# Scalar one-hots, fused sums of expert numbers and a different fill of the query stage, in a hybrid encoder block

## The chip, the cores and the metric

The kernel runs on one core of a Trainium2 chip. The metric is the device time of one execution in microseconds, the median of several runs. The engines go by the names of the profile: PE is TensorE (matmuls), DVE is VectorE, ACT is ScalarE, POOL is GpSimd, and SP issues transfers.

## What is computed

One encoder layer over 512 tokens of width 1024, in fp32:

```python
h = x + mixer(rmsnorm(x, norm_mix_g))       # HGRN2 and Hyena branches, projections, gates
h = h + peer_ffn(rmsnorm(h, norm_ffn_g))
out = rmsnorm(h, norm_final_g)

# peer_ffn, for a block xb of tokens: 8 heads, 2 x 128 sub-keys, 16384 experts
qh = (xb @ w_q).reshape(T, 8, 2, 128)
s = einsum('thpc,hpnc->thpn', qh, subkeys)
s1, i1 = top_k(s[:, :, 0], 16);  s2, i2 = top_k(s[:, :, 1], 16)
cand_s = s1[..., :, None] + s2[..., None, :]          # 256 candidates
cand_i = i1[..., :, None] * 128 + i2[..., None, :]
top_s, pos = top_k(cand_s, 16)
experts = take_along_axis(cand_i, pos);  g = softmax(top_s)
act = gelu(einsum('td,thkd->thk', xb, u_tab[experts])) * g
y = einsum('thk,thkd->td', act, v_tab[experts])
```

## The kernel before

A product of two fp32 matrices is made of three matmuls: each operand is split into a high part (ScalarE, L85) and the rest (a subtraction, L86, on VectorE or GpSimd).

The mixer comes first. `mixer` loads the four blocks of 128 tokens, normalises each (`token_rstd` on ScalarE, a multiplication by the reciprocal root and the weights `gm` on VectorE, L228), and `turn` transposes them with TensorE. `gm` holds the same 1024 weights on all 128 partitions, loaded by one broadcast transfer on SP's queue (L223). ScalarE's queue issues the small tables `vec` and `ident`, and the filter weights `fw3` (L455) and decay rates `decb` (L464) of the Hyena branch. Then follow the Hyena branch, the HGRN2 branch and the output projection, up to about 806 us.

The second half is PEER. Block 0 of the tokens (GTB) has its experts gathered row by row by GpSimd. The other three blocks (DTB) go through all 16384 experts: a row of 128 experts is multiplied with all 384 tokens (`act_row`: 24 matmuls, then gelu), weighted by a dense gate matrix, and multiplied with the same experts' outputs (`combine`: 18 matmuls). The stages are:

1. `queries` (16 halves of heads): a projection, the scores, the 16 best of 128 per token and half head on VectorE (`top16`).
2. `select` (called `chosen`), once for each block and half of the heads: 50 candidate pairs for each of four heads, their 16 best, a softmax, and the expert number of each of the 16 places. A place holds the position of a pair. The expert number is found by comparing the place with the list `pio` of the pairs' positions (L1188), multiplying the one-hot by the candidates' numbers (L1190), and summing (L1181). The first eight places can only be among the first 20 pairs. In steps of two heads this makes 12 wide operations a call. It yields after each step, with a cost that is used for interleaving.
3. `gates_out`, for each of the three blocks: with an expert number split into row and column, every token's 128 choices become two one-hots of 128 x 128, which TensorE multiplies into the token's part of the gate matrix. A batch is four tokens, 32 batches a block. `one` (L1228) compares for row and column at once, in bf16, ScalarE copies the rows in another order (L1230), `own` (L1231) multiplies the columns by the gates. The product goes through `Gs` to the memory `Gd`.
4. `rows`, the expert loop: 128 rows of combination, with the rest of the activation rows spread over the first 120, and the gathered block's choices and gathers (`gathered`) woven in.

Activation rows that are made before the loop ("fill") stay in a ring of 14 rows or, for KEPT pairs, go to memory (`kept`) and come back. There are 2 x KEPT + RING - LEFT of them: 27. In `queries`, two are run at its end. The others are woven into the choices and gate matrices by the yielded costs. Before the loop their low parts are subtracted on VectorE, in the loop on GpSimd (`looping`). In `queries` the first halves of two blocks' choices (EARLY) go along, one step per query from the ninth on, the rest at its end.

The order on each engine is made by a planner when the program is built: it takes instructions by their place in the program as soon as, by its own estimates, their inputs and buffers are there. `issue_after` puts instructions behind a given one on the same engine.

Of the kernel before, what the change touches and what calls it, by code (L numbers as in the profile page):

```python
# [21 lines left out]
P = 128  # L22
L = 512
D = 1024
# [134 lines left out]
def block_kernel(tc, a):  # L159

    nc = tc.nc
    with ExitStack() as ctx:
# [5 lines left out]
        nc.scalar.dma_start(vec, a["vec"])  # L168
# [3 lines left out]
        C = Ctx()  # L172
        C.nc, C.tc, C.a, C.ident, C.ones, C.vec, C.eps = nc, tc, a, ident, ones, vec, epsc
# [28 lines left out]
def mixer(C):  # L202
# [104 lines left out]
def hyena(C, ctx, xh, xl, raws, fill):  # L307
# [112 lines left out]
    for half in range(D // HC):  # L420
# [33 lines left out]
        for row in (0, FH):  # L454
            nc.scalar.dma_start(fw3[row : row + FH], a["f_w3"].rearrange("f (d c) -> f d c", d=2)[:, :, half * HC : half * HC + HC])  # L455
# [6 lines left out]
        for dr in range(2):  # L462
            o = dr * D + half * HC
            nc.scalar.dma_start(decb[:, dr], a["f_decay"][:, o : o + HC].to_broadcast([P, HC]))  # L464
        with tc.issue_after(C.turned):
            nc.scalar.activation(decb, decb, AF.Abs)
# [324 lines left out]
KEPT = 8  # L791
LEFT = 3
UB = 2
EARLY = 2
MIX = 3
STEPS = 1
# [13 lines left out]
def peer(C, ctx, mh, ml):  # L810
# [9 lines left out]
    pio = cp.tile([P, NPAIR, TOPK // 2], BF16, name="pio")  # L820
    with tc.tile_pool(name="pid", bufs=1) as ip:
        pid = ip.tile([P, NPAIR], F32, name="pid")
        nc.scalar.dma_start(pid, a["pair"].to_broadcast([P, NPAIR]))
        nc.vector.tensor_copy(pio, pid[:, :, None].to_broadcast([P, NPAIR, TOPK // 2]))
    iota = cp.tile([P, P, 4], BF16, name="iota")
    nc.gpsimd.iota(iota, pattern=[[1, P], [0, 4]], base=0, channel_multiplier=0, allow_small_or_imprecise_dtypes=True)  # L826
    gidx = cp.tile([P, P], I32, name="gidx")
    gdot = cp.tile([P, P], F32, name="gdot")
    gw = cp.tile([P, P], F32, name="gw")
    def chosen(pool, tb, part, ahead=2):  # L830
        return select(C, pool, tb, part, v16, i16, gate, eid, pio, ahead)
# [53 lines left out]
    with tc.tile_pool(name="slw", bufs=2) as sw, tc.tile_pool(name="gb", bufs=1) as gb, \  # L885
            tc.tile_pool(name="go", bufs=3) as go, tc.tile_pool(name="ps_g", bufs=5, space=PSUM) as ps_g:
        def main():
            rest = [[chosen(sw, tb, part) for part in range(2) if part or k >= EARLY] for k, tb in enumerate(DTB)]
            yield from chain(*rest[0])
            for k, tb in enumerate(DTB):  # L890
                nxt = chain(*rest[k + 1]) if k + 1 < len(DTB) else iter(())
# [245 lines left out]
def select(C, w2, tb, part, v16, i16, gate, eid, pio, ahead=2):  # L1137
# [59 lines left out]
    while found:  # L1197
        reduce()
# [170 lines left out]
```

## Time and profile before

| | us |
|---|---|
| median of 3 runs | 2113.68 (2111.99 to 2114.71) |
| the profiled execution | 2113.9 |
| its span, first to last instruction | 2112.1 |
| PE busy | 2058.7 |
| DVE busy | 1736.1 |
| ACT busy | 978.6 |
| POOL busy | 638.2 |

The span is one execution on the chip. Busy time of an engine is the time in which at least one of its instructions ran; the durations of matmuls are modelled, and a matmul's record overlaps the next, as do the records of VectorE. A timeline row begins with the start in us from the span's start and the time that the row covers; neighbouring instructions of one kind are merged to one row (x2). The difference of two starts is what an instruction costs in a row of others.

### The profile page before, as it was taken

What the parts mean: (1) busy time and instruction counts of PE and PEld (TensorE: products, weight loads), DVE (VectorE), ACT (ScalarE), POOL (GpSimd) and SP (SyncE); (2) the same over time, 40 slices, a digit from 0 to 9 for tenths busy, and PEclk for the clock granted to TensorE, in tenths of its full rate; (3) what the DMA queues carried; (4) which work ended last, traced back from release to release, by engine and by line L of the source; (5) the groups of instructions that cost most, each with busy time, mean ns of one, the idle gap of its engine ahead of it and who ended that gap; (6) DMA issues with size and microseconds to landing.
All of it is one profiled execution on the core that took longest, in us unless ns stands there. A gap on an engine that the chain in (4) does not pass through costs nothing. (4 is left out here: it accounts for less than half of the span.)

```text
span 2112.1 us, 29790 instructions
## 1 busy us (share of the span) xinstructions
PE 2058.7 (97%) x11109; PEld 1822.7 (86%) x11109; DVE 1736.1 (82%) x3073; ACT 978.6 (46%) x1396; POOL 638.2 (30%) x361
## 2 busy tenths in 40 slices
PE   7999999999999999979999999999999999999998
PEld 6888888888888898879988989989989998998997
DVE  6888764998998546999999988878878879778785
ACT  6555434667665623337766423333333333333333
POOL 0000000000000000000000378877777676666760
PEclk9999999999999999999999999999999999999999
DMA  6212222222212444124547689988888988888884
GB/s 199 80 51 66 70 70 94 67 65 66 70 54 81 120 151 139 61 70 168 202 180 250 192 311 344 327 318 304 321 318 301 317 311 299 316 317 324 296 286 148
DMA packets 153949, 407.68 MB, mean 193 GB/s; under 512 B 12457, under 2 KB 65451, under 8 KB 152140
## 3 DMA queue, kind: packets, MB, share of 16 engines
q1 hardware_dynamic: 110028, 255.98, 35.8%
q0 software_dynamic: 36864, 134.23, 17.6%
q10 hardware_dynamic: 6912, 15.56, 2.1%
q8 instruction: 87, 1.43, 0.3%
q14 instruction: 58, 0.48, 0.1%
HBM read 373.22 MB, written 32.51 MB: 192 GB/s over the span
## 5 line engine op out<-in xcount | busy, mean ns | idle before, releaser
L86 POOL TENSOR_TENSOR ul<-uraw,uh 128x1024 fp32r<-128x1024 f32 x100 | 265.3, 2654 | 589.7 <-DMA uraw<-in_uT 387.6
L95 PE MATMUL ps_a<-pxl,uh 128*128 128x384 f32 x1008 | 343.1, 340 | 0.0
L94 PE MATMUL ps_a<-pxh,uh 128*128 128x384 f32 x1008 | 341.8, 339 | 1.3 <-ACT gact L867 1.2
L980 PE MATMUL acc<-vl,gh 128*128 128x512 f32 x768 | 301.5, 393 | 2.1 <-DVE vl L86 2.1
L979 PE MATMUL acc<-vh,gh 128*128 128x512 f32 x768 | 299.7, 390 | 2.6 <-ACT vh L85 2.6
L981 PE MATMUL acc<-vh,gl 128*128 128x512 f32 x768 | 301.5, 393 | 0.0
L94 PE MATMUL ps_mm<-xh,whi 128*128 128x512 f32 (+1 forms) x656 | 259.1, 396 | 1.5 <-ACT xh L195 1.2
L940 DVE SCALAR_TENSOR_TENSOR xg<-grow,gw,xg 128x1024 f32<-128x1024 f32 x127 | 208.6, 1643 | 63.1 <-DMA grow<-in_v,gidx 62.0
L931 DVE SCALAR_TENSOR_TENSOR grow<-grow,xg 128x1024 f32<-128x1024 f32 x128 | 195.9, 1541 | 73.6 <-DMA grow<-in_u,gidx 73.3
L95 PE MATMUL ps_mm<-xl,whi 128*128 128x512 f32 (+1 forms) x656 | 255.0, 390 | 0.3 <-DVE xl L196 0.3
L85 ACT CAST vh<-vraw 128x1024 fp32r<-128x1024 f32 x128 | 134.3, 1050 | 252.7 <-PE acc L981 179.7
L826 POOL IOTA iota<- 128x512 bf16 x1 | 1.2, 1237 | 754.4 <-DVE gt L281 754.4
L906 POOL DMA_INDIRECT grow<-in_u,gidx x128 | 201.0, 1570 | 41.4 <-issue 19.4
L97 PE MATMUL ps_a<-pxh,ul 128*128 128x384 f32 x1008 | 200.1, 338 | 6.3 <-DVE ul L86 4.1
L85 ACT CAST uh<-uraw 128x1024 fp32r<-128x1024 f32 x128 | 134.7, 1053 | 143.5 <-PE ps_a L95 76.5
L94 PEld LDWEIGHTS ps_a<-pxh,uh 128*128 128x128 f32 x1008 | 191.1, 190 | 6.4 <-ACT gact L867 2.2
L95 PEld LDWEIGHTS ps_a<-pxl,uh 128*128 128x128 f32 x1008 | 190.9, 189 | 3.8
L86 DVE TENSOR_TENSOR vl<-vraw,vh 128x1024 fp32r<-128x1024 f32 x128 | 186.4, 1457 | 8.3 <-ACT vh L85 8.3
L97 PEld LDWEIGHTS ps_a<-pxh,ul 128*128 128x128 f32 x1008 | 176.8, 189 | 8.2 <-DVE ul L86 5.5
L906 POOL DMA_INDIRECT grow<-in_v,gidx x128 | 170.5, 1332 | 32.7 <-issue 18.3
L85 ACT CAST whi<-wraw 128x1024 fp32r<-128x1024 f32 x112 | 117.3, 1050 | 131.0 <-PE ps_mm L95 123.5
L980 PEld LDWEIGHTS acc<-vl,gh 128*128 128x128 f32 x768 | 144.6, 188 | 31.1 <-DVE vl L86 2.9
(414 smaller groups left out, 4188.8 us busy)
## 6 DMA issues: line engine op xcount, KB each, us to landing
uraw<-in_uT SPq DMA_DIRECT2D x128, 512.0 KB, 7.0
vraw<-in_v SPq DMA_DIRECT2D x128, 512.0 KB, 6.3
wraw<-in_w_in SPq DMA_DIRECT2D x80, 512.0 KB, 3.6
Gd<-Gs SPq DMA_DIRECT2D x12, 2048.0 KB, 7.2
gt<-Gd SPq DMA_DIRECT2D x32, 768.0 KB, 8.7
wraw<-in_w_q SPq DMA_DIRECT2D x16, 512.0 KB, 4.0
wraw<-in_w_b SPq DMA_DIRECT2D x8, 512.0 KB, 3.6
wraw<-in_w_a SPq DMA_DIRECT2D x8, 512.0 KB, 4.3
```

Of the source, the lines that this page charges most:

```text
L85: nc.scalar.copy(hi, src)
L86: return (eng or nc.vector).tensor_sub(lo, src, hi).ins
L94: nc.tensor.matmul(out, ah, bh, start=(i == 0), stop=False)
L95: nc.tensor.matmul(out, *((al, bh) if late else (ah, bl)), start=False, stop=False)
L97: nc.tensor.matmul(out, *((ah, bl) if late else (al, bh)), start=False, stop=(stop and i == n - 1))
L826: nc.gpsimd.iota(iota, pattern=[[1, P], [0, 4]], base=0, channel_multiplier=0, allow_small_or_imprecise_dtypes=True)
L906: nc.gpsimd.indirect_dma_start(out=t, out_offset=None, in_=tab, in_offset=bass.IndirectOffsetOnAxis(ap=gidx[:, j : j + 1], axis=0))
L931: nc.vector.scalar_tensor_tensor(t, t, 1.0, xg, op0=ALU.mult, op1=ALU.mult, accum_out=gdot[:, j : j + 1])
L940: nc.vector.scalar_tensor_tensor(gacc, t, gw[:, j : j + 1], gacc, op0=ALU.mult, op1=ALU.add)
L979: nc.tensor.matmul(acc[k][:, c], gh[:, ts_], vh[:, ds_], start=(r == 0), stop=False)
L980: nc.tensor.matmul(acc[k][:, c], gh[:, ts_], vl[:, ds_], start=False, stop=False)
L981: nc.tensor.matmul(acc[k][:, c], gl[:, ts_], vh[:, ds_], start=False, stop=(r == NK - 1))
```

## The change

The expert numbers are found by one operation for each of the 64 places of a call: it compares the list of positions with the place (a scalar per token, read through a pointer), multiplies by the candidates' numbers and sums. For that `pio` and `cpf` become fp32. In `gates_out` the bf16 compare is made for the rows alone, and the columns' one-hot times gate by one operation per token with two scalars per partition (number and gate), compared with `line`, the numbers 0 to 127.

KEPT is 10. `queries` runs an activation row after each query from the eighth on, with two choice steps, and takes the first halves of all three blocks. The part of `main` after it begins with the second half of the first block, its costs multiplied by 1.3.

The weights of the first normalisation come as one row of 4 KB on ScalarE's queue, and two matmuls with ones copy it to all partitions of two PSUM banks, from where VectorE reads it, in two halves. `vec` is issued after `ident`, and the transfers of `fw3` and `decb` after the last turned copy.

```diff
-        nc.scalar.dma_start(vec, a["vec"])
         nc.scalar.dma_start(ident, a["ident"])
+        C.fetch_vec = lambda: nc.scalar.dma_start(vec, a["vec"])
...
         log_table(C)
-        gm = n1.tile([P, D], F32, name="gm")
+        C.fetch_vec()
+        gm = n1.tile([1, D], F32, name="gm")
+        gps = [C.ps_x.tile([P, 512], F32, name="ps_x") for _ in range(2)]
...
-                nc.sync.dma_start(gm, a["g_mix"].to_broadcast([P, D]))
+                nc.scalar.dma_start(gm, a["g_mix"])
+                for c, pg in enumerate(gps):
+                    nc.tensor.matmul(pg, C.ones[0:1], gm[:, c * 512 : c * 512 + 512], start=True, stop=True)
...
-            nc.vector.scalar_tensor_tensor(xn, xn, rs, gm, op0=ALU.mult, op1=ALU.mult)
+            for c, pg in enumerate(gps):
+                xc = xn[:, c * 512 : c * 512 + 512]
+                nc.vector.scalar_tensor_tensor(xc, xc, rs, pg, op0=ALU.mult, op1=ALU.mult)
...
-        for row in (0, FH):
-            nc.scalar.dma_start(fw3[row : row + FH], ...)
+        with tc.issue_after(C.turned):
+            for row in (0, FH):
+                nc.scalar.dma_start(fw3[row : row + FH], ...)
...
-        for dr in range(2):
-            o = dr * D + half * HC
-            nc.scalar.dma_start(decb[:, dr], ...)
         with tc.issue_after(C.turned):
+            for dr in range(2):
+                o = dr * D + half * HC
+                nc.scalar.dma_start(decb[:, dr], ...)
...
-KEPT = 8
+KEPT = 10
+FIRSTC = 1.3
-EARLY = 2
-STEPS = 1
+STEPS = 2
...
-            rest = [[chosen(sw, tb, part) for part in range(2) if part or k >= EARLY] for k, tb in enumerate(DTB)]
-            yield from chain(*rest[0])
+            rest = [chosen(sw, tb, 1) for tb in DTB]
+            for c in rest[0]:
+                yield FIRSTC * c
...
-        early = chain(*(chosen(sw, tb, 0) for tb in DTB[:EARLY]))
+        early = chain(*(chosen(sw, tb, 0) for tb in DTB))
-            if hp > 7:
+            if hp >= HEADS - 1:
                 run(islice(early, STEPS))
+                next(fill)
...
-    for hd in range(0, H, H2):
-        for k0, n in ((0, NFIRST), (K2, NPAIR)):
-            one = w2.tile([P, H2, NPAIR, K2], BF16, name="one", bufs=2)
-            ex = w2.tile([P, H2, K2, NPAIR], F32, name="exp", bufs=ahead + 1)
-            nc.vector.tensor_tensor(one[:, :, :n], ..., op=ALU.is_equal)
-            nc.vector.tensor_mul(ex[:, :, :, :n], ...)
-            ...
-            yield 0.7 if k0 == 0 else 1.3
+    for hd in range(H):
+        for k in range(TOPK):
+            n = NFIRST if k < TOPK // 2 else NPAIR
+            own = w2.tile([P, NPAIR], F32, name="own", bufs=4)
+            nc.vector.scalar_tensor_tensor(own[:, :n], pio[:, :n], cpf[:, hd, k : k + 1], ci[:, hd, :n],
+                                           op0=ALU.is_equal, op1=ALU.mult, accum_out=out[:, hd, k : k + 1])
+        yield 0.9
...
-            nc.vector.tensor_tensor(one, iota[:, None].to_broadcast([P, 2, P, 4]),
-                                    tr[:, b, :, None, :].to_broadcast([P, 2, P, 4]), op=ALU.is_equal)
-            nc.scalar.copy(rows, one[:, 0].rearrange("p i t -> p t i"))
-            nc.vector.tensor_tensor(own, one[:, 1].rearrange("p i t -> p t i"),
-                                    tg[:, b * 4 : b * 4 + 4, None].to_broadcast([P, 4, P]), op=ALU.mult)
+            nc.vector.tensor_tensor(one, iota, tr[:, b, None, :].to_broadcast([P, P, 4]), op=ALU.is_equal)
+            nc.scalar.copy(rows, one.rearrange("p i t -> p t i"))
+            for q in range(4):
+                t = b * 4 + q
+                nc.vector.tensor_scalar(own[:, q], line, tg[:, 0, t : t + 1], tg[:, 1, t : t + 1], op0=ALU.is_equal, op1=ALU.mult)
```

## Rows read from the trace of the kernel before

**Rows 1.** The page: busy us, share of the span, instructions.

```profile
PE 2058.7 (97%) x11109; PEld 1822.7 (86%) x11109; DVE 1736.1 (82%) x3073; ACT 978.6 (46%) x1396; POOL 638.2 (30%) x361
```

**Rows 2.** Stretches: busy us of each engine (count), granted PE clock, DMA share, GB/s.

```profile
core 0: us, PE busy (x) PEld busy (x) DVE busy (x) ACT busy (x) POOL busy (x), PEclk, DMA share, GB/s
806.00:850.00 44.00, 41.84 (x232) 35.89 (x231) 34.97 (x161) 16.61 (x28) 0.00 (x0) 0.96 0.42 138
850.00:950.00 100.00, 89.40 (x454) 77.26 (x453) 97.66 (x506) 34.23 (x56) 0.00 (x0) 0.97 0.19 62
950.00:1136.00 186.00, 178.24 (x1236) 169.85 (x1235) 184.39 (x444) 144.19 (x245) 0.00 (x0) 0.97 0.52 190
1136.00:1164.00 28.00, 23.74 (x125) 22.43 (x124) 27.49 (x118) 13.27 (x17) 5.50 (x3) 0.92 0.80 275
1164.00:1250.00 86.00, 83.33 (x404) 74.81 (x402) 77.76 (x148) 31.02 (x39) 45.52 (x22) 0.97 0.69 224
1250.00:2096.00 846.00, 846.00 (x4210) 761.57 (x4209) 687.00 (x602) 299.28 (x355) 585.78 (x332) 1.00 0.86 308
```

**Rows 3.** Timeline of PE in the loop: start us, us, instruction.

```profile
1346.32 0.39 PE L979 MATMUL acc<-vh,gh 128*128 128x512 f32 x1
...
1350.44 0.33 PE L94 MATMUL ps_a<-pxh,uh 128*128 128x384 f32 x1
...
1354.62 0.39 PE L979 MATMUL acc<-vh,gh 128*128 128x512 f32 x1
```

**Rows 4.** Timeline of DVE: the expert numbers of two heads in a choice call.

```profile
916.92 1.56 DVE L1190 TENSOR_TENSOR exp<-one,ci 128x800 f32<-128x800 bf16 x1
...
919.00 0.30 DVE L1188 TENSOR_TENSOR one<-pio,cpf 128x320 bf16<-128x320 bf16 x1
919.22 0.47 DVE L1181 TENSOR_REDUCE eid<-exp 128x16 f32<-128x320 f32 x1
919.62 0.72 DVE L1190 TENSOR_TENSOR exp<-one,ci 128x320 f32<-128x320 bf16 x1
920.25 0.57 DVE L1188 TENSOR_TENSOR one<-pio,cpf 128x800 bf16<-128x800 bf16 x1
920.74 0.98 DVE L1181 TENSOR_REDUCE eid<-exp 128x16 f32<-128x800 f32 x1
```

**Rows 5.** Timeline of DVE: two gate batches.

```profile
1090.56 1.27 DVE L1228 TENSOR_TENSOR one<-iota,tr 128x1024 bf16<-128x1024 bf16 x2
1091.75 1.28 DVE L1231 TENSOR_TENSOR own<-one,tg 128x512 f32<-128x512 bf16 x2
```

**Rows 6.** Timeline of DVE: operations with one scalar per partition (`omlb`, `edec`).

```profile
356.22 0.75 DVE L640 SCALAR_TENSOR_TENSOR KQ<-raw,omlb,so 128x512 f32<-128x512 f32 x1 [0.44 <-ACT so L636]
...
371.05 0.34 DVE L697 SCALAR_TENSOR_TENSOR S<-S,edec,ps_x 128x128 f32<-128x128 f32 x1
371.31 0.42 DVE L713 TENSOR_TENSOR KM<-KQ,Dt 128x256 f32<-128x256 f32 x1
```

**Rows 7.** Timeline of DVE: scalar operations, with two pointers (L375) and with none.

```profile
65.67 0.81 DVE L375 TENSOR_SCALAR arg<-ps_x,vec 64x512 f32<-64x512 f32 x1 [3.47 <-PE ps_x L389]
...
949.21 0.21 DVE L1211 TENSOR_SCALAR i<-i 128x128 f32<-128x128 f32 x1
```

**Rows 8.** Timeline of DVE: an operation with an accumulated sum, in the loop.

```profile
1310.14 1.21 DVE L931 SCALAR_TENSOR_TENSOR grow<-grow,xg 128x1024 f32<-128x1024 f32 x1
1311.28 0.08 DVE L931 DVE_READ_ACCUMULATOR grow<-grow,xg 128x1 f32 x1
1311.28 3.40 DVE L931 SCALAR_TENSOR_TENSOR grow<-grow,xg 128x1024 f32<-128x1024 f32 x1
```

**Rows 9.** Groups from 806 to 1136 us: count, busy us, mean ns, idle before.

```profile
L86 DVE TENSOR_TENSOR ul<-uraw,uh 128x1024 fp32r<-128x1024 f32 x27 | 32.7, 1211 | 2.2 <-ACT uh L85 2.2
```

**Rows 10.** The first projection on PE; transfers of the filter weights (issue to landing).

```profile
14.93 0.58 PE L94 MATMUL ps_mm<-xh,whi 128*128 128x256 f32 x1 [1.16 <-ACT xh L195]
...
fw<-in_f_w ACTq DMA_DIRECT2D x8, 128.0 KB, 3.0
```

More of the change, by code (lines that the diff above doesn't have):

```diff
@@ L453, in hyena @@
         fw3 = w2.tile([2 * FH, 2, HC], F32, name="fw3", bufs=1)
-        for row in (0, FH):
-            nc.scalar.dma_start(fw3[row : row + FH], a["f_w3"].rearrange("f (d c) -> f d c", d=2)[:, :, half * HC : half * HC + HC])
+        with tc.issue_after(C.turned):
+            for row in (0, FH):
+                nc.scalar.dma_start(fw3[row : row + FH], a["f_w3"].rearrange("f (d c) -> f d c", d=2)[:, :, half * HC : half * HC + HC])
         fw3h = w2.tile([2 * FH, 2, HC], F32R, name="fw3h", bufs=1)
@@ L461, in hyena @@
         decb = w2.tile([P, 2, HC], F32, name="decb", bufs=1)
-        for dr in range(2):
-            o = dr * D + half * HC
-            nc.scalar.dma_start(decb[:, dr], a["f_decay"][:, o : o + HC].to_broadcast([P, HC]))
         with tc.issue_after(C.turned):
+            for dr in range(2):
+                o = dr * D + half * HC
+                nc.scalar.dma_start(decb[:, dr], a["f_decay"][:, o : o + HC].to_broadcast([P, HC]))
             nc.scalar.activation(decb, decb, AF.Abs)
@@ L819, in peer @@
     i16 = cp.tile([P, TB, 16, TOPK], U32, name="i16")
[L820 to L824, printed above, removed]
+    pio = cp.tile([P, NPAIR], F32, name="pio")
+    nc.scalar.dma_start(pio, a["pair"].to_broadcast([P, NPAIR]))
     iota = cp.tile([P, P, 4], BF16, name="iota")
     nc.gpsimd.iota(iota, pattern=[[1, P], [0, 4]], base=0, channel_multiplier=0, allow_small_or_imprecise_dtypes=True)
+    line = cp.tile([P, P], F32, name="line")
+    nc.gpsimd.iota(line, pattern=[[1, P]], base=0, channel_multiplier=0, allow_small_or_imprecise_dtypes=True)
     gidx = cp.tile([P, P], I32, name="gidx")
@@ L829, in peer, with chosen @@
     gw = cp.tile([P, P], F32, name="gw")
-    def chosen(pool, tb, part, ahead=2):
-        return select(C, pool, tb, part, v16, i16, gate, eid, pio, ahead)
+    def chosen(pool, tb, part):
+        return select(C, pool, tb, part, v16, i16, gate, eid, pio)
     projected(C, mh, ml, xh, xl, xg)
@@ L916, in gathered @@
                     yield 3.2
-            yield from chosen(sw, GTB, part, 1)
+            yield from chosen(sw, GTB, part)
         sgctx.close()
@@ L1134, with select @@
            for x in range(a0, a0 + na) for y in range(b0, b0 + nb)]
-def select(C, w2, tb, part, v16, i16, gate, eid, pio, ahead=2):
+def select(C, w2, tb, part, v16, i16, gate, eid, pio):
     nc = C.nc
@@ L1211, in gates_out @@
     nc.vector.tensor_scalar(i1, i1, 1.0 / 128, None, op0=ALU.mult)
-    tr = gb.tile([P, P // 4, 2, 4], BF16, name="tr", bufs=2)
-    tg = gb.tile([P, P], F32, name="tg", bufs=2)
+    tr = gb.tile([P, P // 4, 4], BF16, name="tr", bufs=2)
+    tg = gb.tile([P, 2, P], F32, name="tg", bufs=2)
     pt = ps_g.tile([P, 512], F32, name="ps_g")
@@ L1217, in gates_out @@
         nc.tensor.transpose(pt[:, j * P : j * P + P], src, C.ident)
-    nc.scalar.copy(tr.rearrange("p b j t -> p j b t"), pt[:, : 2 * P].rearrange("p (j b t) -> p j b t", j=2, t=4))
-    nc.scalar.copy(tg, pt[:, 2 * P : 3 * P])
+    nc.scalar.copy(tr, pt[:, :P].rearrange("p (b t) -> p b t", t=4))
+    nc.scalar.copy(tg, pt[:, P : 3 * P].rearrange("p (j t) -> p j t", j=2))
     NB = P // 4
```

26 lines of the change are left out of this document (6 added, 20 removed).

## The prediction

> **What bounds the kernel now.** I read the page's engine table first. TensorE is busy for 97% of the span and VectorE for 82% [rows 1], so an average names TensorE. Then I cut the span into stages, because an average hides where a different engine decides. In the expert loop (1250 to 2096 us) TensorE is never idle: 846.00 of 846 us [rows 2]. There, time is the number of matmuls. One expert row of activations (24 matmuls of 384 columns) and one row of combination (18 of 512) take 1346.32 to 1354.62 us, 8.30 us, of which the 24 take 4.18 [rows 3]. Before the loop it is the other way round. In the three stretches from 806 to 1136 us (queries, choices, gate matrices) VectorE is busy 317.0 of 330 us, and from 850 on 282.1 of 286. TensorE is idle there for 2.2 + 10.6 + 7.8 = 20.5 us, and its granted clock averages 0.96 to 0.97 in these stretches, since each pause is followed by one at 1.2 instead of 2.4 GHz. By these shares that is worth another 0.04 x 44 + 0.03 x 100 + 0.03 x 186 = 10 us at most [rows 2]. So up to 1136 us VectorE sets the pace, and TensorE could take some 31 us more of work for nothing. After 1136 us the gate matrices go to memory and back, and TensorE is idle for 4.3 us until the loop has its first rows [rows 2].
>
> Whoever wants to gain must therefore take work from VectorE before 1136 us, or carry activation rows (TensorE's work) from the loop into that stage. The change does the second for certain. Whether it does the first is the question.
>
> **Four activation rows more ahead of the loop.** KEPT 10 for 8 makes the fill 2 x 10 + 14 - 3 = 31 rows instead of 27, so the loop has four fewer: 4 x 4.18 = 16.7 us less TensorE time where TensorE is the bound [rows 3]. In the earlier stage they cover idle TensorE time, of which there is enough. Each also brings a low-part subtraction to VectorE, 1.21 us recorded (27 of them there now [rows 9]) and 1.14 from start to start, since a VectorE record overlaps the next by some 0.07 us. That is 4 x 1.14 = +4.6 us on the engine that binds. In the loop GpSimd does this subtraction. The two more kept pairs are written from ScalarE's queue and read back on SP's; the loop's other transfers hide them, and without that cover I have no more than two waits of DMA there. A row per later query and two choice steps only change where this work stands: TensorE gets rows in the 10.6 us in which it now waits for choices, but as long as VectorE is full, the end of the stage doesn't move for that.
>
> **Expert numbers by fused sums.** Now two heads cost six wide operations, step by step from start to start: one 0.22, sum 0.40, product 0.63, one 0.49, and by duration less the overlap product 1.48 and sum 0.90: 4.12 us, so 8.2 us for a call of four heads [rows 4]. Afterwards a call has 64 operations: 32 over 20 pairs, 32 over 50, each with a per-token scalar read through a pointer and an accumulated sum. The price of a pointer: the same operation with one took 371.05 to 371.31 = 0.26 us for 128 elements, and 0.75 recorded, some 0.67 from start to start, for 512 [rows 6]; without one, 512 elements take 0.60 (two `own` in 1091.75 less the next start, 1.28 recorded for two [rows 5]). Fitting 1.04 ns an element, the fixed part is 0.13 us with a pointer and 0.07 without. So 0.15 us for 20 and 0.18 for 50 elements: 32 x 0.33 = 10.6 us a call, +2.4. Six calls stand before 1136 us: +14 us. The accumulated sum I take as free: behind 1024 elements the read of the accumulator is recorded at 1311.28 and the next operation starts at 1311.28 too [rows 8]. If each read took a slot of its own 0.08 us, a call would cost 5.1 more, six of them 31. If the pointer were hidden, 32 x (0.09 + 0.12) = 6.7 us, six calls -9.
>
> A rule speaks against this part. In the rows the accumulating operation with two fp32 inputs takes 1.14 us for 1024 elements, as much as 1024 elements without a sum: 1.14 by rows 9 less the overlap [rows 8, 9]. The Trainium skill, Vector Engine (DVE) Microarchitecture Reference, Points that are easy to get wrong, says that the form with two non-bf16 SBUF sources runs at half rate because no port is left for the accumulator. By that rule (an estimate) the sums would be dearer by one pass; the trace does not agree.
>
> **One-hot rows by scalars.** Per batch of four tokens VectorE now does two operations of about 0.60 us: 1.20 [rows 5]. The 1024-element compare becomes 512: at the same rate 0.07 + 0.27 = 0.34 us. The product becomes four operations of 128 elements, each with two pointers. Without pointers such a scalar operation over 128 fp32 elements is recorded at 0.21, less the overlap some 0.13, which is half a cycle an element: 0.07 + 128 x 0.52 ns [rows 7]. Two pointers: the only operation with two, 512 elements from PSUM, took 0.81 us [rows 7] where a plain one of 512 is recorded at 0.68 (1.28 for two less one step of 0.60 [rows 5]); so 0.11 to 0.13 for both. I take 0.24 each, 0.96 for four, 1.30 in all: +0.10 a batch, and with 96 batches +9 us. Hidden pointers would give 0.34 + 0.52 = 0.86, -33 us in all; a whole cycle (1.04 ns) an element would add 4 x 0.067 x 96 = 26.
>
> **Start.** TensorE's first projection starts at 14.93 us, after waiting 1.16 us for ScalarE's turned input [rows 10]. The weights' 512 KB broadcast leaves SP's queue, so the later blocks of x and the first weights move up one place on it; the 4 KB row goes to ScalarE's queue behind `ident` and `vec`. Two small matmuls then wait for it, and the first normalisation on VectorE waits for them; behind it there stand the second block's normalisation and the low parts, for which TensorE waits. Halves let transposes start half an operation sooner. `vec`, two `fw3` and two `decb` transfers are issued later on ScalarE's queue, the last four behind the last turned copy; a transfer of this size lands 3.0 us after its issue [rows 10], and ScalarE, which works in order, may stand that long at `fw3h` with a weight cast behind it. Bounds -3 and +3 us; I take -1, as removing 512 KB ahead of x is the larger part.
>
> **Sum.** VectorE before 1136: +14 + 9 + 4.6 = +28 us; the loop -16.7; the start -1. The two calls for the gathered block (+5 us) stand at 1136 to 1250, where VectorE has 8.7 us idle and TensorE 6.9 [rows 2]; I take 0, at worst +5. So +10 us on the profiled execution's 2113.9 (span 2112.1 and 1.8 around it, 0.2 above the median 2113.68): 2124 us, with 2114 to 2136 by the smaller bounds.
>
> **Rivals.**
> Pointers hidden (the faster side): if a pointer is fetched while the operation before still runs, VectorE loses 33 + 9 - 4.6 = 37 us. Then TensorE binds before 1136: its 309.5 us of work less 10 at the low clock plus 16.7 are 316 of 330, so the stage gains some 10 to 14, the loop 16.7, the start 1: 2082 to 2086, and 2091 when only half is hidden. Against it: each row with a pointer is dearer. For it: these rows are of single operations between others, not of long runs alike. There are 6 x 64 + 96 x 8 = 1152 pointers at 0.057 us, and the point from which it decides is near: +28 falls under 17.7, break-even, if a pointer costs 0.048. Chance 0.21; a price of 0.035 to 0.05 (2099 to 2116) another 0.16.
> Accumulator reads take a slot: +31, 2155; against it, the equal starts [rows 8]. 0.07.
> The four scalar operations take a whole cycle an element: +26, 2150; against it the 0.13 us [rows 7]. 0.07.
> Sums at half rate: 32 x 70 x 1.04 ns = 2.3 us a call, six +14: 2138; the trace is against it [rows 8]. 0.02. This is the rule named above.
> The new work falls into VectorE's 9 us of idle time before 850 [rows 2], since rows and choices begin a query earlier: 2115. 0.05. That the four rows find no gap, and the change so doesn't do what it says, would cost their 16.7 us again (2141); with some 31 us free in that stage I give it no chance of its own.
>
> **How the numbers follow.** The forecast has 0.42. A measurement tells 0.2%, 4.2 us, from no change: faster is under 2109.5, slower over 2117.9. Faster: 0.21 and 0.12 of the 0.16, 0.33. Same: 0.04 of it, 0.07 of the forecast, 0.05: 0.16. Slower: 0.35 + 0.07 + 0.07 + 0.02 = 0.51. The range 2086 to 2152 leaves out about half of the hidden pointers and of the dear reads, some 0.15. The likeliest sign's own range is 2118 to 2152.
>
> **What would show it.** A choice call's 64 sums at 0.15 and 0.18 us from start to start, with the next start on the accumulator's read; `own` steps near 0.24; VectorE full from 850 us to the last gate batch, and that batch later by some 28 us (at 1164 rather than 1136); the loop's stretch shorter by 16 to 17 us with TensorE full; TensorE's first projection near 14. The forecast is wrong if the steps are under 0.13 and 0.19, or if TensorE rather than VectorE is full before the loop.

## The result, and the profile after

The changed kernel takes 2133.32 us (median of 4 runs, 2132.69 to 2135.35) beside 2114.19 us of the kernel before on the same chip: ratio 1.0094, 95% interval [1.0076, 1.0111]. It is slower by 19 us, where 10 were forecast. Its profiled execution took 2135.35 us, the span of it 2133.6.

The engine table of after, beside [rows 1]: TensorE has the same work (4 matmuls more, for `gm`), VectorE 24.7 us more, and GpSimd 21 less.

```profile
PE 2059.6 (97%) x11113; PEld 1821.8 (85%) x11113; DVE 1760.8 (83%) x4296; ACT 990.2 (46%) x1400; POOL 617.1 (29%) x358
```

The stretches of after over the same times as [rows 2] (from, to, length, then busy us of each engine with its count, granted PE clock, DMA share, GB/s):

```profile
core 0: us, PE busy (x) PEld busy (x) DVE busy (x) ACT busy (x) POOL busy (x), PEclk, DMA share, GB/s
806.00:850.00 44.00, 39.47 (x229) 34.89 (x228) 31.12 (x140) 16.77 (x30) 0.00 (x0) 0.92 0.44 144
850.00:950.00 100.00, 94.08 (x486) 81.87 (x485) 99.80 (x740) 40.71 (x62) 0.00 (x0) 1.00 0.27 86
950.00:1136.00 186.00, 170.61 (x1094) 162.17 (x1092) 183.91 (x1080) 118.85 (x193) 0.00 (x0) 0.96 0.45 161
1136.00:1164.00 28.00, 26.67 (x197) 24.61 (x195) 28.00 (x93) 23.87 (x42) 2.46 (x1) 1.00 0.43 169
1164.00:1250.00 86.00, 74.26 (x416) 67.41 (x415) 84.91 (x394) 44.63 (x64) 20.56 (x8) 0.96 0.74 245
```

VectorE is as full as forecast: 311.7 of 314 us from 850 to 1164. But the last gate batch does not stand at 1164: it stands at 1185.6, against 1131.9 before. TensorE is idle 15.4 us from 950 to 1136, twice as long as before.

The steps that the prediction priced, in VectorE's timeline (start, us, instruction; neighbours of one kind merged). A gate batch, its `one` and four `own`, to be read beside [rows 5]:

```profile
1019.26 0.43 DVE L1223 TENSOR_TENSOR one<-iota,tr 128x512 bf16<-128x512 bf16 x1
1019.60 1.13 DVE L1227 TENSOR_SCALAR own<-line,tg 128x128 f32<-128x128 f32 x4
1020.62 1.24 DVE L86 TENSOR_TENSOR ul<-uraw,uh 128x1024 fp32r<-128x1024 f32 x1
```

The compare steps 0.34 us, four `own` 1.02, so 0.256 each: 1.36 us a batch instead of 1.20. And the sums, beside [rows 4]:

```profile
1025.28 0.11 DVE L1191 DVE_READ_ACCUMULATOR own<-pio,cpf,ci 128x1 f32 x1
1025.28 0.26 DVE L1191 SCALAR_TENSOR_TENSOR own<-pio,cpf,ci 128x20 f32<-128x20 f32 x1
1025.44 0.11 DVE L1191 DVE_READ_ACCUMULATOR own<-pio,cpf,ci 128x1 f32 x1
1025.44 0.29 DVE L1191 SCALAR_TENSOR_TENSOR own<-pio,cpf,ci 128x50 f32<-128x50 f32 x1
1025.63 0.11 DVE L1191 DVE_READ_ACCUMULATOR own<-pio,cpf,ci 128x1 f32 x1
1025.63 0.29 DVE L1191 SCALAR_TENSOR_TENSOR own<-pio,cpf,ci 128x50 f32<-128x50 f32 x1
```

A sum over 20 pairs takes 0.16 us, over 50 pairs 0.19, and the next one starts when the accumulator is read, as behind the long sums of [rows 8]. A call is 32 x 0.352 = 11.3 us instead of 8.2 [rows 4]; six calls, +18 us.

TensorE's first projection starts at 14.56 us instead of 14.93 [rows 10], behind the two weight matmuls and the turned block (start, us, instruction, idle time before and what ended it):

```profile
7.06 3.75 PE L227 MATMUL ps_x<-gm,ones 1*128 1x512 f32 x4 [7.06 <-DMA gm<-in_g_mix]
10.74 4.00 PE L192 MATMUL ps_x<-ident,xn 128*128 128x128 f32 x16
14.56 0.53 PE L94 MATMUL ps_mm<-xh,whi 128*128 128x256 f32 x2
```

Set up as four terms, from the first matmul of the query scores (818.4 us before, 826.0 after), the last gate batch (1131.9, 1185.6), and the first and the last matmul of the combination (1158.7 to 2104.2, 1213.1 to 2125.4): everything ahead of the queries +7.6, the stage from there to the last gate batch 313.5 to 359.6, +46.1, the way to the first combination +0.7, the loop 945.5 to 912.3, -33.2. That is +21.2 on the profiled executions. The forecast had -1, +28, 0 and -16.7.

### The profile page after: what moved, and what is told of

It is laid out like the page before. It is cut to its first block, busy times and chain, and to the rows that moved or that the text cites. A ratio compares the mean times of both kernels' runs of the same rounds, so it can differ in the third digit from the quotient of the medians.

```text
span 2133.6 us, 30906 instructions
## 1 busy us (share of the span) xinstructions
PE 2059.6 (97%) x11113; PEld 1821.8 (85%) x11113; DVE 1760.8 (83%) x4296; ACT 990.2 (46%) x1400; POOL 617.1 (29%) x358
## 3 DMA queue, kind: packets, MB, share of 16 engines
q1 hardware_dynamic: 110172, 256.24, 35.4%
## 4 chain that ended last, share of the span: by engine, by line
PE 67%; DVE 25%; ACT 4%; DMA 2%; issue 2%; POOL 0%; ACTq 0%; DVEq 0%; SPq 0%; POOLq 0%
PE acc L987 7%; PE acc L986 7%; PE acc L988 7%; PE ps_mm L97 7%; PE ps_mm L94 7%; PE ps_mm L95 7%; PE ps_a L97 6%; PE ps_a L95 6%; PE ps_a L94 6%; DVE own L1191 5%; DVE own L1227 4%; PE ps_x L725 1%; DVE wlo L86 1%; DVE ul L86 1%; DVE one L1223 1%
## 5 line engine op out<-in xcount | busy, mean ns | idle before, releaser
L86 POOL TENSOR_TENSOR ul<-uraw,uh 128x1024 fp32r<-128x1024 f32 x96 | 249.5, 2599 | 625.9 <-DVE one L1223 396.0
L94 PE MATMUL ps_a<-pxh,uh 128*128 128x384 f32 x936 | 317.9, 340 | 7.4 <-ACT gact L873 7.4
L95 PE MATMUL ps_a<-pxl,uh 128*128 128x384 f32 x936 | 317.4, 339 | 0.0
L938 DVE SCALAR_TENSOR_TENSOR grow<-grow,xg 128x1024 f32<-128x1024 f32 x128 | 205.5, 1624 | 66.5 <-DMA grow<-in_u,gidx 66.4
L947 DVE SCALAR_TENSOR_TENSOR xg<-grow,gw,xg 128x1024 f32<-128x1024 f32 x127 | 195.5, 1539 | 45.7 <-DMA grow<-in_v,gidx 44.4
L97 PE MATMUL ps_a<-pxh,ul 128*128 128x384 f32 x936 | 185.6, 338 | 9.1 <-POOL ul L86 8.8
L94 PEld LDWEIGHTS ps_a<-pxh,uh 128*128 128x128 f32 x936 | 177.2, 189 | 12.0 <-ACT gact L873 8.3
L95 PEld LDWEIGHTS ps_a<-pxl,uh 128*128 128x128 f32 x936 | 177.3, 189 | 3.5
L986 PEld LDWEIGHTS acc<-vh,gh 128*128 128x128 f32 x768 | 144.6, 188 | 36.2 <-ACT vh L85 9.2
L86 DVE TENSOR_TENSOR wlo<-wraw,whi 128x1024 fp32r<-128x1024 f32 x112 | 136.7, 1221 | 45.3 <-PE ps_mm L97 22.3
```

The costliest lines, as they stand in the source:

```text
L86: return (eng or nc.vector).tensor_sub(lo, src, hi).ins
L94: nc.tensor.matmul(out, ah, bh, start=(i == 0), stop=False)
L95: nc.tensor.matmul(out, *((al, bh) if late else (ah, bl)), start=False, stop=False)
L97: nc.tensor.matmul(out, *((ah, bl) if late else (al, bh)), start=False, stop=(stop and i == n - 1))
L938: nc.vector.scalar_tensor_tensor(t, t, 1.0, xg, op0=ALU.mult, op1=ALU.mult, accum_out=gdot[:, j : j + 1])
L947: nc.vector.scalar_tensor_tensor(gacc, t, gw[:, j : j + 1], gacc, op0=ALU.mult, op1=ALU.add)
```

## What the experiments measured

TensorE's work is the same in all kernels here, to a few matmuls. The time in which it is idle from the first scores matmul until 100 us past the first matmul of the combination (the length less the busy time of two rows of stretches) therefore should move with the time of the kernel. It is the column "lost"; its differences follow those of the time to within 8 us, so it shows which way a run went and not the last few us. It comes from the one profiled execution of each run, and work at a lower granted clock counts as busy in it. Ratios are to the kernel before, run on the same chip; not all runs were on one chip, so between two runs the ratios are the better comparison.

| run | us | ratio [95%] | lost, us |
|---|---|---|---|
| before | 2112 to 2114 | 1 | 25.4 |
| after | 2133.3 | 1.0094 [1.0076, 1.0111] | 43.2 |
| after, positions loaded early (e1) | 2130.1 | 1.0081 [1.0066, 1.0095] | 40.6 |
| after, wide choices and early load (e2) | 2123.2 | 1.0044 [1.0030, 1.0058] | 31.3 |
| after, wide gate batches (e3) | 2122.0 | 1.0040 [1.0025, 1.0054] | 37.3 |
| after, both wide: fill and start remain (e4) | 2116.8 | 1.0016 [1.0002, 1.0030] | 33.2 |
| before, KEPT 10 (e5) | 2111.1 | 0.9997 [0.9988, 1.0007] | 24.8 |
| before, query fill (e6) | 2129.9 | 1.0085 [1.0066, 1.0103] | 45.3 |
| after, constants for `own` (e7) | 2110.0 | 0.9987 [0.9977, 0.9997] | 27.2 |
| after, GpSimd late (e8) | 2134.5 | 1.0109 [1.0091, 1.0127] | 40.2 |
| e3, GpSimd late (e9) | 2115.7 | 1.0015 [1.0006, 1.0025] | 31.5 |
| e6, GpSimd late (e10) | 2112.8 | 0.9996 [0.9986, 1.0005] | 30.9 |
| e9, positions early (e11) | 2112.2 | 0.9999 [0.9990, 1.0009] | 29.8 |
| before, both small forms (e12) | 2134.4 | 1.0109 [1.0092, 1.0126] | 41.9 |
| e4, GpSimd late (e13) | 2109.7 | 0.9983 [0.9973, 0.9992] | 26.1 |
| before, fused sums (e14) | 2126.0 | 1.0058 [1.0042, 1.0075] | 35.3 |
| before, scalar `own` (e15) | 2126.6 | 1.0069 [1.0053, 1.0086] | 32.7 |

### The small forms by themselves

The first theory is the prediction's: VectorE sets the pace ahead of the loop, so what the small forms add there reaches the end in whole. The rival is that TensorE uses the longer stage for rows that then leave the loop.

e12 puts both small forms into the kernel before (`pio` loaded early), and e14 and e15 one each:

```diff
+            nc.vector.scalar_tensor_tensor(own[:, :n], pio[:, :n], cpf[:, hd, k : k + 1], ci[:, hd, :n],
+                                           op0=ALU.is_equal, op1=ALU.mult, accum_out=out[:, hd, k : k + 1])
...
+                nc.vector.tensor_scalar(own[:, q], line, tg[:, 0, t : t + 1], tg[:, 1, t : t + 1], op0=ALU.is_equal, op1=ALU.mult)
```

> The kernel before with both small forms (fused sums, four scalar operations per gate batch) and nothing else of the change; the pair positions are loaded early. VectorE gets 17 us more in the choices and 15 to 21 more in the gates. If VectorE alone sets the pace up to the last gate batch, as the prediction has it, the time is 2146 to 2152. If TensorE fills part of the longer stage with rows, which then leave the loop, about half or less passes through: 2122 to 2133.

> The kernel before with the fused sums alone (old gate batches, old fill, positions loaded early). VectorE gets some 17 us more in six calls ahead of the loop. If VectorE's time passes to the end by about half, as it did with both forms (21 of some 38 us), 2120 to 2123. If the choices stand where TensorE is filled by rows anyway, less: 2113 to 2118. If it all passes: 2130.

> The kernel before with the four scalar operations per gate batch alone (wide choices, old fill). VectorE gets 96 x 0.16 = 15 us more, with no GpSimd subtraction beside them in that stage. At half that passes on, 2119 to 2123; if all passes, 2128; if the gates are what the 21 us of both forms came from, 2126 to 2134.

Measured: sums 2126.0 (+13.4), gates 2126.6 (+13.9), both 2134.4 (+21.2). By the steps VectorE got 18 us for the sums and 96 x 0.16 = 15 for the gates, 33 together. So some two thirds arrive: between the two theories, and 1 us above the rival's range. Each alone arrives for more than the half that was expected. In e12 the stage is 34.1 us longer and the loop 14.4 shorter. TensorE's account of before and then of e12 (first scores matmul to the first combination, and 100 us from there):

```profile
818.40:1158.70 340.30, 319.20 (x1963) 293.01 (x1961) 332.62 (x1212) 197.64 (x334) 4.86 (x2) 0.97 0.43 154
1158.70:1258.70 100.00, 95.70 (x454) 85.41 (x455) 91.76 (x163) 37.80 (x47) 53.91 (x26) 0.95 0.71 233
```

```profile
817.60:1193.10 375.50, 334.59 (x1987) 301.24 (x1985) 371.63 (x2278) 204.09 (x337) 7.17 (x3) 0.97 0.38 138
1193.10:1293.10 100.00, 98.99 (x486) 88.67 (x487) 94.04 (x321) 38.55 (x47) 53.85 (x29) 0.98 0.79 271
```

TensorE gets 24 matmuls, one row, more into a stage that is 35 us longer, and starts its first 100 us of loop better supplied (32 matmuls more). It loses 16.5 us more in all; the time grew by 21.2. These two forms alone make the change slower.

Where TensorE stands longer can be read from its waits from the first scores matmul on (engine, line, what ended the wait, us in total, times, longest), before (818 to 1132 us) and then e12 (818 to 1180 us):

```profile
PE ps_a L97 <- DVE ul L86: 4.1, 4, 1.5
```

```profile
PE ps_g L1227 <- ACT rows L1218: 16.5, 16, 3.0
PE ps_a L97 <- DVE ul L86: 12.8, 12, 6.1
```

L97 is an activation row's last third, which needs the low part. In e12 one such subtraction starts on VectorE at 933.34 us, behind a run of sums that began at 922.86. This wait is 12.2 us in e14, with the sums alone, and 4.4 in e15. The gate products wait for ScalarE's copy of `one`, 1.7 us before, 16.5 in e12 and 10.5 in e15.

The price of the pointers is measured with the scalars of `own` as constants (e7), the numbers and gates then being absent from the gate matrix:

```diff
-                nc.vector.tensor_scalar(own[:, q], line, tg[:, 0, t : t + 1], tg[:, 1, t : t + 1], op0=ALU.is_equal, op1=ALU.mult)
+                nc.vector.tensor_scalar(own[:, q], line, float(t), 0.01, op0=ALU.is_equal, op1=ALU.mult)
```

> The changed kernel with the four operations per gate batch taking two constants in place of two scalars per partition; the tokens' expert columns and gates are left out of the gate matrix by that. If the pointers are what makes the operation 0.256 us (steps without a pointer were 0.13), the step falls to 0.13 to 0.15 and a batch by 0.4 to 0.5 us, VectorE loses 40 to 48 us before the loop, and the time falls by 10 us (as much as the wide form gave back) up to 25: 2108 to 2123. If pointers are hidden and the operation simply costs that, the step stays at 0.25 and the time at 2133.

VectorE's timeline in e7 shows four such operations in 0.54 us (1041.83 to 1042.37), 0.135 each:

```profile
1041.83 0.62 DVE L1227 TENSOR_SCALAR own<-line 128x128 f32<-128x128 f32 x4
1042.37 0.24 DVE L1163 TENSOR_TENSOR ci<-i1x,i16f 128x16 f32<-128x16 f32 x2
```

Two pointers therefore cost 0.256 - 0.135 = 0.12 us an operation, and 384 operations 46 us of VectorE. The kernel took 2110.0 us, 23 less than after: half of those 46 us arrived. The operation itself is the cheap one (0.135 against 0.60 / 4 = 0.15 of the wide product); the pointers make it dear.

### The wide forms in the changed kernel

e2, e3 and e4 put the wide choices, the wide gate batches, and both back into the changed kernel (e2 and e4 with `pio` loaded early, as the wide form had it):

```diff
-            nc.vector.tensor_tensor(one, iota, tr[:, b, None, :].to_broadcast([P, P, 4]), op=ALU.is_equal)
+            nc.vector.tensor_tensor(one, iota[:, None].to_broadcast([P, 2, P, 4]), tr[:, b, :, None, :]..., op=ALU.is_equal)
+            nc.vector.tensor_tensor(own, one[:, 1].rearrange("p i t -> p t i"), tg[...].to_broadcast([P, 4, P]), op=ALU.mult)
```

> The changed kernel with the expert numbers found by the six wide operations per two heads again (and with them the early load of the pair positions, as in e1). Theory 1 (VectorE binds ahead of the loop; a call of 64 sums costs 11.2 us against 8.3): 6 x 2.9 = 17 us less VectorE work there on top of e1, so 2108 to 2115. Rival (the added time is hidden by TensorE's fill rows, or comes from elsewhere): as e1, 2125 to 2129.

> The changed kernel with gates_out as before: one compare of 1024 elements and one product of 512 for a batch instead of one compare of 512 and four scalar operations. Theory 1: VectorE loses 96 x 0.22 = 21 us ahead of the loop (four steps of 0.256 and one of 0.335 against 1.20, and three scalar operations that stood for 2.3 us beside GpSimd's subtraction); some rows that now fit ahead of the loop no longer do, so 2112 to 2120. Rival (four small operations let the matmuls start earlier and only the sums cost time): 2130 to 2136.

> Both wide forms again, with the changed fill (KEPT 10, a row and two steps per later query) and the changed start. Theory 1 (the sums and scalars cost 43 us of VectorE, the fill gains): VectorE has only the 4.6 us of four more subtractions more than before, the loop 16.7 us less: 2092 to 2104, faster than the 2114 of the kernel before. Rival (TensorE has no room ahead of the loop, so the four rows come back there): 2110 to 2116.

Measured: 2123.2, 2122.0 and 2116.8 us. The first two lie between the theory and its rival, the third 1 us above the rival's range. With both wide forms, what remains of the change (fill and start) should by the prediction have been 13 us faster than before; it was 3.6 slower. So the fill did not bring its 16.7 us, and e3 brought 11 us, where its gate batches take 21 us off VectorE (96 x 0.16, and 6 us of waits beside GpSimd, below). e5 and e6 divide the fill, on the kernel before; the factor 1.3 on the first costs is in neither, only in the runs with the whole fill.

### Four rows more: KEPT 10 alone

```diff
-KEPT = 8
+KEPT = 10
```

> The kernel before with four rows more in memory ahead of the loop (KEPT 10) and nothing else of the change. By the sum of the prediction the loop loses 4 x 4.18 = 16.7 us, VectorE gets 4.6 us in the stage before, so about 2102 us. By the rival (the idle time of TensorE ahead of the loop is made of waits between two engines that each row also has to sit out, and rows put there lengthen the stage by their own time) the stage from the first score to the last gate batch grows by some 17 us with TensorE's idle time of about 18 us unchanged, and the time stays at 2112 to 2117.

2111.1 us, ratio 0.9997 [0.9988, 1.0007]: nothing. The stretches of e5 (queries, choices, gate batches, then up to the first combination, and 100 us of loop) show where the rows went; those of before are the second fence:

```profile
818.60:914.90 96.30, 93.20 (x470) 76.97 (x469) 90.94 (x510) 31.70 (x60) 0.00 (x0) 1.00 0.22 70
914.90:953.40 38.50, 30.81 (x158) 29.67 (x157) 38.50 (x173) 14.78 (x21) 0.00 (x0) 0.91 0.29 100
953.40:1131.20 177.80, 168.58 (x1193) 160.09 (x1193) 177.15 (x405) 139.71 (x238) 0.00 (x0) 0.99 0.53 197
1131.20:1183.00 51.80, 48.36 (x268) 47.96 (x267) 50.96 (x153) 26.29 (x35) 13.95 (x4) 0.93 0.75 251
```

```profile
818.40:915.40 97.00, 93.88 (x469) 77.68 (x468) 91.44 (x515) 31.64 (x60) 0.00 (x0) 0.99 0.21 66
915.40:953.20 37.80, 30.22 (x157) 28.94 (x157) 37.80 (x169) 14.85 (x21) 0.00 (x0) 0.91 0.29 101
953.20:1131.90 178.70, 170.94 (x1196) 162.55 (x1195) 177.15 (x405) 139.85 (x238) 0.00 (x0) 0.98 0.52 192
1131.90:1158.70 26.80, 24.17 (x146) 23.85 (x144) 26.23 (x128) 11.30 (x17) 4.86 (x2) 1.00 0.85 290
```

Up to the last gate batch the two are alike, with the same matmuls to within three and nearly the same idle time of TensorE (20.0 us, before 18.5). All the additional rows stand behind it: 268 matmuls instead of 146, 51.8 us instead of 26.8, and the loop is 28.8 us shorter (945.5 to 916.7). Work went from one place where TensorE is nearly full to another. The idle time ahead of the last batch was not touched: the program takes a row from the fill whenever the steps that it has yielded add up to a fixed cost (`PER`), and rows beyond those come at the end. No run changed `PER`, so whether rows set closer would have covered that idle time is open. The time followed the lost time (24.8 against 25.4), not the length of the loop.

### Rows and choices in the queries

```diff
-EARLY = 2
-STEPS = 1
+EARLY = 3
+STEPS = 2
...
-            if hp > 7:
+            if hp >= HEADS - 1:
                 run(islice(early, STEPS))
+                next(fill)
```

> The kernel before with the other half of the changed fill alone: an activation row after each query from the eighth on, two choice steps with it, first halves of all three blocks; KEPT stays 8 and all operations stay wide. By the prediction this only moves where the work stands: 2112 to 2116. By the rival (a row between two queries delays the projection that the next scores wait for, so that VectorE, which the queries keep full, gets idle time there) VectorE's idle time in the stage grows by 10 us or more over 7.3 and the time is 2118 to 2126.

2129.9 us, +18, worse than the rival had it. But most of the idle time did not stand between the queries. The longest piece stands at 1133 us, in the gate batches (waits of e6 from 1110 to 1165 us: engine, line, what ended the wait, us in total, times, longest):

```profile
PEld ps_g L1239 <- ACT rows L1231: 16.4, 4, 13.9
PE ps_g L1239 <- ACT rows L1231: 15.2, 2, 13.6
DVE one L1229 <- ACT rows L1231: 14.3, 2, 13.1
ACT Gs L1244 <- DMA Gd<-Gs: 14.1, 1, 14.1
```

TensorE and VectorE stand for ScalarE, and ScalarE for a store of the gate matrix. SP's queue in that time (1112 to 1152 us), then GpSimd's timeline:

```profile
SPq L846 <- POOL ul L86: 29.8, 2, 28.8
```

```profile
1118.13 21.99 POOL L86 TENSOR_TENSOR ul<-uraw,uh 128x1024 fp32r<-128x1024 f32 x2 [9.54 <-PE ps_a L97]
```

The fill was used up early (its rows were run in the queries), so the loop's first rows began while gate batches still ran. Their subtraction is GpSimd's, and beside wide gate batches two of them took 22 us, where 2.4 us each is usual; the first alone took 19.69. A load on SP's queue needed the buffer that GpSimd was reading and waited 28.8 us; the store stood behind it on the same queue. The same chain stands in e3: one subtraction of 18.45 us, SP waiting 25.8 us, ScalarE 13.8 for the store. The GpSimd operation in e3, with VectorE's last wide operations ahead of its end:

```profile
1141.21 18.45 POOL L86 TENSOR_TENSOR ul<-uraw,uh 128x1024 fp32r<-128x1024 f32 x1 [385.16 <-ACT uh L85]
```

```profile
1155.58 1.29 DVE L1224 TENSOR_TENSOR own<-one,tg 128x512 f32<-128x512 bf16 x2
1156.78 0.69 DVE L1221 TENSOR_TENSOR one<-iota,tr 128x1024 bf16<-128x1024 bf16 x1
1170.19 0.69 DVE L1221 TENSOR_TENSOR one<-iota,tr 128x1024 bf16<-128x1024 bf16 x1 [12.73 <-ACT rows L1223]
```

VectorE issued wide operations without a pause until 1157.47; GpSimd ended at 1159.66, 2.2 us later, which is about its own duration. In e6 it is the same: GpSimd's first subtraction, and VectorE's last wide operation ahead of its pause:

```profile
1118.13 19.69 POOL L86 TENSOR_TENSOR ul<-uraw,uh 128x1024 fp32r<-128x1024 f32 x1 [9.54 <-PE ps_a L97]
```

```profile
1134.95 0.67 DVE L1229 TENSOR_TENSOR one<-iota,tr 128x1024 bf16<-128x1024 bf16 x1
```

VectorE paused at 1135.62, GpSimd ended at 1137.82, again 2.2 us later. So in both runs the subtraction stood, some 16 and 17 us, until VectorE paused. The Trainium skill, SBUF — State Buffer, SBUF: two separate sides, says that VectorE and GpSimd share a pair of ports as an exclusive lock, and that the loser blocks fully. The trace agrees, and adds that GpSimd got no turn between VectorE operations that follow each other at once. That it is these ports for which it stood is the page's reason; the runs show the standing and its end.

e8, e9, e10, e11 and e13 take the overlap away: the first four subtractions of the loop's rows go to VectorE, so GpSimd begins after the last gate batch.

```diff
-        ins = split(nc, uh, ul, raw, nc.gpsimd if looping else None)
         if looping:
+            looping.append(True)
+        late = len(looping) > 5
+        ins = split(nc, uh, ul, raw, nc.gpsimd if late else None)
+        if late:
             anchor[0] = ins
```

> The kernel before with the changed fill of the queries alone, as in the earlier run, and the first four subtractions of the loop's rows on VectorE. In the earlier run the same stall stood at 1133 us (ScalarE waited 14.1 us for a store of the gate matrix). If the stall is the cost of the query fill, the time falls from 2130 to 2114 to 2118. If rows between queries cost TensorE's time as such, it stays above 2123.

> The changed kernel with the wide gate batches, as in the earlier run with wide gates, and the first four subtractions of the loop's rows on VectorE instead of GpSimd. In the earlier run GpSimd's one subtraction took 18.45 us beside wide batches, a load on SP's queue stood behind it, a store of the gate matrix behind that, and ScalarE waited 13.8 us for the store. If that stall hid what the wide batches give, the stall goes and the time falls by 9 to 14 us to 2108 to 2113. If the wide batches give only what was seen, the time stays at 2118 to 2123.

The query fill fell from 2129.9 to 2112.8, to no difference from before. So the stall was its whole cost, and beside the wide forms rows between queries cost nothing and bring nothing. Its stretches (queries, choices, gate batches) show the exchange:

```profile
817.80:953.60 135.80, 129.46 (x662) 112.08 (x661) 126.80 (x637) 52.91 (x84) 0.00 (x0) 0.97 0.29 92
953.60:991.50 37.90, 30.70 (x176) 29.69 (x174) 37.09 (x178) 16.60 (x23) 0.00 (x0) 0.99 0.37 116
991.50:1145.10 153.60, 150.68 (x1102) 147.99 (x1103) 148.87 (x287) 127.19 (x225) 0.00 (x0) 0.97 0.53 198
```

The queries get 38.8 us longer for eight rows (193 matmuls) and 35.4 us of VectorE's work; TensorE was busy 93.88 of 97 us there before, so there had been no room for a row. The gate batches get 25 us shorter. e9 fell from 2122.0 to 2115.7, between the two expectations: against the stall of 13.8 us that went, there are 4.6 us of the four subtractions more on VectorE.

> The changed kernel with both wide forms and the first four subtractions of the loop's rows on VectorE: what is left of the change is the fill (KEPT 10, a row and two steps per later query) and the start. If the four rows bring what the prediction gave them and only a stall had hidden it, 2098 to 2104. If rows ahead of the loop lengthen the stage there by what the loop saves, as KEPT 10 alone did, 2109 to 2116.

Without small forms and overlap, fill and start give 2109.7 us, 0.9983 [0.9973, 0.9992] of before: some 3 us, where the prediction had 13. TensorE loses 26.1 us, before 25.4. It is 7 us faster than e4, although no store was waited for in e4 and GpSimd's subtraction ahead of the last gate batch took only 4.69 us there; where e4 spends those 7 us is not shown. e13 is the fastest version here.

> The changed kernel with wide gate batches, GpSimd's first four subtractions on VectorE, and the pair positions loaded into a tile of their own at the early place that they had before. That should add the 3 us that the early load gave when it was put into the changed kernel alone: 2105 to 2110, ahead of the kernel before if the sums cost less at the end than the more rows and the start give; 2112 to 2118 if the sums' 17 us on VectorE pass through for more than half.

2112.2 us, level with before: wide gates, early positions and the fill pay for the fused sums, no more.

These runs also show that a part has no price by itself. With the old fill the sums cost 13.4 us (e14). With the changed fill, wide gates and GpSimd late they cost 3 (e11 beside e13). The waits point at the reason: TensorE stood 12.2 us for low parts in e14, 0.2 in e11 and 0.3 in after. So the changed fill, worth 3 us beside the wide forms, is worth more beside the sums. In the company of both small forms, which it has in after, e12 and e1 differ by fill and start alone: 2134.4 and 2130.1 us, ratios 1.0109 and 1.0081, so it brought 4 to 6 us.

### GpSimd beside scalar operations

In after, GpSimd has three subtractions before the last gate batch (1151.83, 1165.52, 1180.25 us). At each, one `own` took 2.3 us. VectorE's row and GpSimd's:

```profile
1151.70 3.19 DVE L1227 TENSOR_SCALAR own<-line,tg 128x128 f32<-128x128 f32 x4
```

```profile
1151.83 2.46 POOL L86 TENSOR_TENSOR ul<-uraw,uh 128x1024 fp32r<-128x1024 f32 x1 [395.98 <-DVE one L1223]
```

Four operations take 3.19 us instead of 1.13. Here GpSimd took 2.46 us, as usual, and VectorE waited, the reverse of e3.

> The changed kernel with the first four subtractions of the loop's rows on VectorE, so that GpSimd has none while gate batches still run. If GpSimd's subtraction is what holds VectorE's scalar operation, the three operations of 2.3 us vanish (longest step of the four-token operations under 0.7 us), VectorE gains 6.2 us less 3 x 1.2 for the subtractions, and the time is 2129 to 2133. If the three long operations come from something else (a transfer, the clock) they stay, and the time is 2133 to 2138.

In e8 the longest of the 384 operations is recorded at 0.35 us, where after has 2.42: the cause is right. The time did not follow: 2134.5 against 2133.3 us. The expectation of 2129 to 2133 was missed; VectorE saved 6.2 us (three times 3.19 - 1.13) and paid 4.6 for the four subtractions, and a difference of that size can't be told here.

### The pair positions

In after, `pio` is loaded straight into a tile of the second half, and the load is issued only at 754 us, which I take for the time at which the tile's memory comes free. ScalarE's queue (start, us, instruction) then has two loads ahead of the residual block `h`, which before was first, at 753.3 us:

```profile
754.33 0.34 ACTq L828 DMA_DIRECT2D pio<-in_pair  x1
754.69 0.55 ACTq L1071 DMA_DIRECT2D gfn<-in_g_ffn  x1
755.27 0.93 ACTq L1076 DMA_DIRECT2D h<-in_x  x2
```

VectorE then waits for `h` (waits of after, 749 to 826 us):

```profile
DVE h L1081 <- DMA h<-in_x: 7.7, 2, 6.5
```

e1 loads them into a tile of its own at the early place and copies them:

```diff
-    nc.scalar.dma_start(pio, a["pair"].to_broadcast([P, NPAIR]))
+    with tc.tile_pool(name="pid", bufs=1) as ip:
+        pid = ip.tile([P, NPAIR], F32, name="pid")
+        nc.scalar.dma_start(pid, a["pair"].to_broadcast([P, NPAIR]))
+        nc.vector.tensor_copy(pio, pid)
```

> The changed kernel with the pair positions loaded into a tile of their own, as before, ahead of the output projection, and copied to pio on VectorE. Theory 1 (the load of pio waits for its memory until 754 us and stands on ScalarE's queue ahead of the residual block h, so VectorE waits 6.5 us for h and TensorE behind it): the first score of the queries comes at 819 to 822 us instead of 826, and the time falls by 4 to 8 us, 2125 to 2129. Rival (the delay comes from the order of h and g_ffn alone, or the stage is shifted without effect because VectorE's backlog is what counts): within 2 us of 2133.

2130.1 us, 3.2 less than after, and the queries start at 821.8 instead of 826.0 us. The start is as expected; the time is 1 us short of the 4 to 8 expected, above the rival's 2, and as the intervals of the two ratios overlap, it is the weakest of the differences here. Of the waits for `h`, 7.7 us in after, 1.1 us is left (e1, 749 to 822 us):

```profile
DVE h L1084 <- DMA h<-in_x: 1.1, 1, 1.1
```

## Why the forecast had the right sign and half the size

**VectorE bounds the stage.** Right for the small forms: VectorE is full in after, and its added work arrives for two thirds (e12). Wrong as a statement on TensorE, whose idle time the prediction then took for free room. The reason that it gave for the low clock there is too wide, too: not each pause was followed by a stretch at 1.2 GHz. From 850 to 950 us of after TensorE is idle for 5.9 us, and the granted clock of the stretch is 1.00, the level of 2.4 GHz.

**Four rows.** This is the step that failed: "In the earlier stage they cover idle TensorE time, of which there is enough", and with it "I give it no chance of its own" for the rival in which the rows find no gap. They found little. KEPT 10 alone brought 1 us (e5), the query fill 0 (e10), both with the start 3 (e13), and in the company of the small forms 4 to 6 (e12 to e1), where -16.7 + 4.6 - 1 = -13 stood in the sum. The idle time was a total over a stretch; where the rows would stand was not asked. From the first scores to the last gate batch it was 18.5 us: 7.6 in 38 us of choices, 7.8 in the gate batches, and 3 in the queries, where rows were sent.

**Fused sums.** Forecast 0.15 and 0.18 us, measured 0.16 and 0.19; +18 us instead of +14. The accumulator's read is free, as [rows 8] said. The rival of half rate is not borne out: 30 elements more cost 0.03 us, 1.07 ns each, where the prediction's fit had 1.04.

**Gate batches.** The compare is right (0.34), the scalar operation was put at 0.24 and takes 0.256; 384 times that is 6 of the 15 us, where 9 were forecast. Three waits for GpSimd added 6.2 on VectorE, for which the sum had no term. The pointers' price, 0.12 us for two, was within the bounds of 0.11 to 0.13; the rival of hidden pointers is out.

**Low parts.** 32 instead of 28 subtractions on VectorE, as forecast.

**The later load of `pio`.** Not in the sum at all: +3 us.

**Start.** First projection 0.4 us earlier; -1 was forecast, and no run separates it.

**The sum again.** The runs lead from before to after in three steps: small forms (before to e12) +21.2, fill and start (e12 to e1) -4.2, the late load (e1 to after) +3.2, together +20 (by the ratios +1.09%, -0.28% and +0.13%); measured +19.1. The forecast had +23, -13 and 0. The price of the small forms was nearly right at the end, which is luck, by two errors that cancel: 33 us of VectorE instead of 23, and a third of it that did not arrive. What doubled the loss is the 7 to 9 us of the fill that did not come. The loop did get shorter, by 33 us and not 16.7, but only because TensorE had made 36 rows instead of 28 (counted by their gelus) when the combination began, so a shorter loop proved nothing.

## What to carry to other kernels

Where one engine's work is fixed, price a move of its work by the idle intervals that it will fill, one by one and at the place where the order puts it; a stage's total of idle time is no such place, and a shorter loop is no gain if the stage ahead of it grew. Measure a part in the company in which it will stand: the sums cost 13 us with one fill and 3 with the other. Before wide operations are replaced by many small ones, price each scalar pointer: here 0.06 us each, which turned an operation of 0.135 us into 0.256. When work for GpSimd slides beside a VectorE stage, look at both engines' longest operation and at what stands behind them on a queue.

## What the runs showed of the hardware

A GpSimd subtraction that takes 2.4 us took 18.45 us (e3) and 19.69 us (e6) beside uninterrupted VectorE operations with two inputs, and ended 2.2 us after their pause both times. The other way round, a VectorE operation of 0.256 us with pointers took 2.3 us beside GpSimd's (after). An accumulating operation with a pointer over 20 elements takes 0.16 us from start to start, and its read costs no slot (after). An operation over 128 elements with a compare and a product takes 0.256 us with two pointers and 0.135 us with two constants in their place (after, e7).
